# A hybrid attention layer on one core: the low parts of the in-projection's weights moved from GpSimd to VectorE

## The chip, the cores and the metric

The kernel runs on one core of one Trainium2 chip. The metric is device time in microseconds of one execution; a time given for a kernel is the median of its runs. The engines are TensorE (PE for matmuls, PEld for weight loads), VectorE (DVE), ScalarE (ACT), GpSimd (POOL) and SyncE (SP, which only issues DMAs here).

## The reference, cut to what matters

One layer of a diffusion backbone over 1024 latent tokens and 256 context tokens, model width 1024. One input projection feeds a gated DeltaNet group (four heads of 128) and a neighbourhood-attention group (eight heads of 64); both go through one output projection, a gated residual and a SwiGLU MLP.

```python
h = modulate(rms_norm(x, w1), shift1, scale1)        # latent and context tokens: T = 1280 rows of 1024
p = h @ w_in                                         # ONE combined in-projection: q, k, v, z, gates | q, k, v
oA = gated_deltanet(p[..., :DN_IN], conv_w, ...)     # short_conv + SiLU on q/k/v, chunked scan both ways
oB = neighbourhood_attention(p[..., DN_IN:], ...)    # QK RMSNorm, window keys + all context keys
x = x + gate1 * (concat(oA, oB) @ w_out)
x = x + gate2 * swiglu(modulate(rms_norm(x, w2), shift2, scale2))
```

Every large product is in float32, made on TensorE as three products of a reduced type: a number is split into a high part (the value rounded to the matmul's type) and a low part (the rest), and high·high, high·low and low·high are summed in PSUM. So each weight must be split once before TensorE can use it: one cast and one subtraction over the tile.

## The kernel before, in words

**Stages.** The profile shows four: the start and the normalization with the first two blocks of the in-projection (0 to 35 us), the rest of the in-projection with the preparation of the DeltaNet chunks running between it (35 to 560 us), the scans and the attention (560 to 780 us), and the output projection with the MLP (780 to 1509 us). The change is in the second.

**The in-projection** is a list of jobs (lines 1073 to 1082), taken in order by one loop (line 1095 on): the blocks k0 and k1 (computed together during the normalization), k2, k3, the wide tile z1, nk0 to nk2, the wide tile nv0, nk3, q0 to q3, nq0 to nq3, v0, the wide tile nv1, v1 to v3, and the wide tile z0. A `Block` makes 128 output columns for 1280 tokens (q and nq: 1024): for each of eight k-tiles, the three products in the order hi·hi, hi·lo, lo·hi (`mm_part`, L419), so the low part of the weights is needed only by the third group of matmuls of a block. A `Wide` tile makes 256 or 272 columns, token tile by token tile (L615).

**A block's weights.** `Block.prefetch` (L430) calls `load` (L191): a DMA on SP's queue into `wraw`, a cast on ACT into `whi` (L203), and `wlo = wraw - whi` (L204) on the engine `lo_engine`. There is one `wraw` buffer in this stage, and two each of `whi` and `wlo`. The next DMA waits until the subtraction has read `wraw`. The loop calls `jobs[n + 1].prefetch()` at the start of job n. A wide tile's weights go through the same `wraw` in two halves (L601 to L608): DMA, cast on ACT (L607), subtraction (L608, 128 x 1024 or 128 x 1088) into `zw`. Before the change GpSimd does 18 of the subtractions L204 and 8 of L608 in this stage. The block k0 names VectorE for its low part and k1 names GpSimd, in both kernels; the loads of the output projection name VectorE, in both.

**What else uses these engines.** VectorE does the short convolution: for the first four k blocks straight from PSUM (L461, accumulator `cacc`), after that from a copy in SBUF (L471, L475). It does the query-key norms (L516, L522, L529), the modulation's sums over DMA'd weights (`modulation`, L236 and L238 into `acc2`, which TensorE then reduces at L223), the recursion that inverts the diagonal blocks of all chunks (`block_inverses`, 30 steps of L916 and L918 on `N`; TensorE transposes `N` in and out at L906 and L928), and parts of the chunk preparation (`prep`: L1017, L1043). GpSimd does the diagonal extractions of the k blocks (L572 into `kd`, L577), the right-hand sides `rc` of the decay matrices (L871, used by TensorE at L884), and `rg` for the chunk preparation (L994, used at L1006).

**What sets the order.** The kernel is written in Tile: each engine's instruction order within the program is chosen by a scheduler that estimates when operands are ready, and semaphores are placed from it. So an instruction that changes its engine also changes where its neighbours stand, on all engines. Each engine runs its instructions strictly in order.

Of the kernel before, what the change touches and what calls it, by code (L numbers as in the profile page):

```python
# [9 lines left out]
F32 = mybir.dt.float32  # L10
# [4 lines left out]
OP = mybir.AluOpType  # L15
# [5 lines left out]
KT = 8  # L21
# [67 lines left out]
def hybrid(ctx, tc, a, dbg):  # L89
    nc = tc.nc  # L90
    pe, act, dve, pool, sp = nc.tensor, nc.scalar, nc.vector, nc.gpsimd, nc.sync
# [96 lines left out]
            dve.scalar_tensor_tensor(r, y, 1.5, r, op0=OP.add, op1=OP.mult)  # L188

    def weights(wp, raws=2, wide=132):  # L190
        def load(src, kt=KT, n=128, lo_engine=pool, raw=None, hi_engine=None):  # L191
            given = raw is not None
            if not given:
                raw = wp.tile([128, KT, wide], F32, name="wraw", tag="wraw", bufs=raws)
            hi = wp.tile([128, KT, 128], F32R, name="whi", tag="whi")
            lo = wp.tile([128, KT, 128], F32R, name="wlo", tag="wlo")
            r, h, o = raw[:, :kt, :128], hi[:, :kt], lo[:, :kt]
            if not given:
                sp.dma_start(r, src)
            if hi_engine:  # L200
                hi_engine.tensor_copy(h, r)
            else:
                act.copy(h, r)  # L203
            lo_engine.tensor_tensor(o, r, h.bitcast(F32), OP.subtract)  # L204
            return h, o
        return load
# [182 lines left out]
    with ExitStack() as bs:  # L389
# [32 lines left out]
        class Block:  # L422
# [4 lines left out]
                self.segs = SEGS[1:] if kind in ("q", "nq") else SEGS  # L427
                self.t0 = self.segs[0][0]

            def prefetch(self, raw=None, lo_engine=pool, hi_engine=None):  # L430
                i = self.i
                src = {"q": lambda: a["w_conv"][i], "k": lambda: a["w_conv"][4 + i], "v": lambda: a["w_conv"][8 + i],
                       "nq": lambda: a["w_nqk"][i], "nk": lambda: a["w_nqk"][4 + i]}[self.kind]()
                self.w = load_w(src, lo_engine=lo_engine, raw=raw, hi_engine=hi_engine)
# [149 lines left out]
        class Wide:  # L584
# [10 lines left out]
            def prefetch(self):  # L595
                h2, n = 2 * self.half, self.n // 2
                src = a["w_nv"] if self.kind == "nv" else a["w_z%d" % self.half]
                if self.kind == "z":
                    h2 = 0
                self.room()  # L600
                for i in range(2):  # L601
                    raw = wp.tile([128, KT, 136], F32, name="wraw", tag="wraw", bufs=1)
                    r, s = raw[:, :, :n], slice(i * n, i * n + n)
                    q = sp if self.half or self.kind == "nv" else act
                    with tc.issue_after(jobs[-3].last.ins) if i and q is act else ExitStack():
                        q.dma_start(r, src[h2 + i])
                        act.copy(self.hi[:, :, s], r)  # L607
                    pool.tensor_tensor(self.lo[:, :, s], r, self.hi[:, :, s].bitcast(F32), OP.subtract)  # L608

            def wide(self, t, c0, c1):  # L610
                p = bank("blk")
# [580 lines left out]
    with ExitStack() as gs:  # L1192
# [18 lines left out]
        def load(d, c, near):  # L1211

            def tile_of(name, src):
                t = sl.tile([128, 4, 128], F32, name=name, tag=name)
                sp.dma_start(fl(t), src)
                return t

            both = shared.pop(c, None)
            if both is None:
                r = slice(c * 128, (c + 1) * 128)  # L1220
                both = [tile_of("v", v_d[r]), tile_of("kt", k_d[r])]
                y = tile_of("y", fl(y_d[d, c]))
                both += [tile_of("kT", fl(kT_d[:, c])), tile_of("qT", fl(qT_d[:, c - 2])) if c >= 2 else None]
                if c in near:
                    shared[c] = both
            else:
                y = tile_of("y", fl(y_d[d, c]))
            at = tile_of("at", fl(at_d[d, c - 2])) if c >= 2 else None
            v, kt, kT, qT = both
            ready[d, c] = kT, qT, kt, v, y, at  # L1230
# [599 lines left out]
```

## Time and profile before

| | before |
|---|---|
| three runs | 1507.06, 1509.69, 1513.23 us (median 1509.69) |
| the profiled execution | 1510.77 us; its span 1509.0 us |
| PE busy in the span | 1458.9 us (97%) |
| DVE busy | 993.4 us (66%) |
| ACT busy | 704.0 us (47%) |
| POOL busy | 237.5 us (16%), 200 of them before 560 us |

How to read it: "busy" is the time in which the engine ran an instruction, so an instruction that is held up while it runs counts as busy for longer. A row of a group of instructions gives line, engine, operation, output and inputs, and durations in nanoseconds. A row of the waits names the engine, tile and line that waited, then the releaser, then the total, the count and the longest. A row of the timeline gives start, duration, engine, line, operation and operands, and in brackets the idle time ahead of it and what ended that.

### The profile page before, as it was taken

To read this page: it belongs to the slowest core of one execution; us is meant where nothing else is said; L and a number is where in the kernel's file an instruction comes from. 1 tells how busy PE (TensorE), PEld (TensorE's weight loads), DVE (VectorE), ACT (ScalarE), POOL (GpSimd) and SP (SyncE) were. 2 spreads that over 40 slices of the span, in tenths; PEclk is the share of its full clock that TensorE was granted. 3 is DMA by queue.
4 is the path that set the end of the run, shared out by engine and by line. 5 is a ranking of instruction groups with operands and counts; after the bars stand their busy time and mean duration, and the time that the engine had idled before them with its cause. 6 is when DMAs were issued, how large, how long until landed. Compare 5 with 4: busy or idle time off the path is not lost.

```text
span 1509.0 us, 23906 instructions
## 1 busy us (share of the span) xinstructions
PE 1458.9 (97%) x8702; PEld 1222.2 (81%) x8702; DVE 993.4 (66%) x1716; ACT 704.0 (47%) x1389; POOL 237.5 (16%) x286
## 2 busy tenths in 40 slices
PE   6999999999999998999999999999999999999998
PEld 3788797877788887888878888888888888888887
DVE  5773589865463745779867489765555567598652
ACT  5443442456663246667843284333333334354440
POOL 1154501455652201112210000000000000000000
PEclk9999999999999999999999999999999999999999
DMA  9274132778665558999539205333333335798742
GB/s 385 79 220 138 57 83 64 248 211 248 189 195 185 157 164 289 300 261 293 166 119 338 76 28 174 134 105 105 105 105 105 105 105 174 271 349 279 251 140 84
DMA packets 205398, 267.36 MB, mean 177 GB/s; under 512 B 15968, under 2 KB 113760, under 8 KB 204256
## 3 DMA queue, kind: packets, MB, share of 16 engines
q1 hardware_dynamic: 197680, 260.01, 53.5%
q10 hardware_dynamic: 7600, 5.81, 1.2%
q8 instruction: 69, 1.13, 0.3%
q14 instruction: 49, 0.40, 0.1%
HBM read 201.02 MB, written 68.94 MB: 179 GB/s over the span
## 4 chain that ended last, share of the span: by engine, by line
PE 51%; ACT 1%; DVE 1%; issue 0%; DVEq 0%
PE ps L1404 28%; PE ps L1747 14%; PE ps L1533 3%; PE ps L1381 1%; PE ps L1555 1%; PE sc L322 1%; PE sc L332 1%; PE sc L309 1%; DVE bt L313 0%; ACT sq L1308 0%; PE ps L1258 0%; ACT oacc L1325 0%; PE ps L223 0%; PE ps L1279 0%; PE ps L1284 0%
## 5 line engine op out<-in xcount | busy, mean ns | idle before, releaser
L1465 ACT CAST uhi<-wq 128x512 fp32r<-128x512 f32 x101 | 61.3, 622 | 135.4 <-issue 84.6
L419 PE MATMUL blk<-hh,whi 128*128 128x512 f32 (+1 forms) x410 | 121.2, 389 | 1.5 <-ACT kk L568 1.4
L1465 ACT CAST uhi<-ws 128x512 fp32r<-128x512 f32 x91 | 53.9, 621 | 146.6 <-PE ps L1404 92.1
L615 PE MATMUL blk<-zw,hh 128*128 128x256 f32 (+1 forms) x576 | 113.2, 291 | 1.0 <-ACT cr L467 1.0
L419 PE MATMUL blk<-hl,whi 128*128 128x512 f32 (+1 forms) x410 | 113.4, 370 | 0.3 <-DVE hl L735 0.3
L419 PE MATMUL blk<-hh,wlo 128*128 128x512 f32 (+1 forms) x410 | 112.5, 371 | 0.6 <-POOL wlo L204 0.6
L1466 DVE TENSOR_TENSOR ulo<-wq,uhi 128x512 fp32r<-128x512 f32 x101 | 67.6, 687 | 59.1 <-ACT uhi L1465 32.8
L1404 PE MATMUL ps<-hT,uhi 128*128 128x512 f32 x336 | 103.7, 390 | 0.0
L1404 PE MATMUL ps<-lT,uhi 128*128 128x512 f32 x336 | 103.5, 389 | 0.0
L1404 PE MATMUL ps<-hT,ulo 128*128 128x512 f32 x336 | 103.4, 389 | 0.0
L615 PEld LDWEIGHTS blk<-zw,hh 128*128 128x128 f32 x576 | 91.5, 190 | 4.2 <-ACT cr L467 1.4
L1404 PE MATMUL ps<-hB,uhi 128*128 128x512 f32 x288 | 89.1, 390 | 0.0
L1404 PE MATMUL ps<-lB,uhi 128*128 128x512 f32 x288 | 88.8, 389 | 0.0
L1404 PE MATMUL ps<-hB,ulo 128*128 128x512 f32 x288 | 88.6, 389 | 0.0
L419 PEld LDWEIGHTS blk<-hh,wlo 128*128 128x128 f32 x410 | 71.2, 189 | 14.8 <-POOL wlo L204 0.9
L419 PEld LDWEIGHTS blk<-hl,whi 128*128 128x128 f32 x410 | 71.3, 189 | 14.3 <-DVE hl L735 0.8
L615 PE MATMUL blk<-zw,hl 128*128 128x256 f32 (+1 forms) x288 | 82.3, 286 | 0.0
L419 PEld LDWEIGHTS blk<-hh,whi 128*128 128x128 f32 x410 | 67.9, 190 | 16.7 <-issue 3.8
L204 POOL TENSOR_TENSOR wlo<-wraw,whi 128x1024 fp32r<-128x1024 f32 x18 | 44.8, 2491 | 185.1 <-ACT whi L203 178.8
L1404 PEld LDWEIGHTS ps<-lT,uhi 128*128 128x128 f32 x336 | 63.1, 188 | 13.2
L1404 PEld LDWEIGHTS ps<-hT,ulo 128*128 128x128 f32 x336 | 63.1, 188 | 13.1
L1404 PEld LDWEIGHTS ps<-hT,uhi 128*128 128x128 f32 x336 | 62.9, 188 | 12.9
(361 smaller groups left out, 3499.3 us busy)
## 6 DMA issues: line engine op xcount, KB each, us to landing
wq<-w_fo SPq DMA_DIRECT2D x99, 256.0 KB, 4.4
wq<-w_gu SPq DMA_DIRECT2D x88, 256.0 KB, 2.9
wad<-wa SPq DMA_DIRECT2D x64, 256.0 KB, 4.2
bt<-rpb SPq DMA_DIRECT2D x64, 192.0 KB, 4.0
t_d<-g SPq DMA_DIRECT2D x22, 512.0 KB, 3.5
fr<-t_d SPq DMA_DIRECT2D x44, 256.0 KB, 4.9
f_d<-g SPq DMA_DIRECT2D x33, 256.0 KB, 2.1
fr<-f_d SPq DMA_DIRECT2D x33, 256.0 KB, 4.4
```

Source lines behind the costliest of these rows:

```text
L204: lo_engine.tensor_tensor(o, r, h.bitcast(F32), OP.subtract)
L309: s = pe.matmul(sc[:, u * 640 + n0:u * 640 + n1], q, ks[i], start=i == 0, stop=i == 1)
L322: pe.transpose(sc[:, u * 640 + j * 128:u * 640 + (j + 1) * 128], bt[:, j * 128:(j + 1) * 128], ident)
L332: return pe.matmul(sc[u * ND:u * ND + ND, 1280:1408], vv, pts[u][:, j * 128:(j + 1) * 128], start=j == 0, stop=j == 4)
L419: pe.matmul(o, ww[:, k], xx[k][:, s], start=k == 0 and j == 0, stop=k == KT - 1 and j == 2)
L615: pe.matmul(p[:, :c1 - c0], x[k][:, s], ww[:, k, c0:c1], start=k == 0 and j == 0, stop=k == KT - 1 and j == 2)
L1381: pe.matmul(o, w[wi][:, k], parts[xi][k][:, s], start=k == 4 and j == 0, stop=k == 3 and j == 2)
L1404: pe.matmul(o, w[wi][:, k], x[xi][:, k], start=first and k == 0 and j == 0, stop=k == n - 1 and j == 2, skip_group_check=True)
L1465: act.copy(hi, self.raw[key])
L1466: dve.tensor_tensor(lo, self.raw[key], hi.bitcast(F32), OP.subtract)
L1533: pe.matmul(o, w[wi][:, k], parts[xi][k][:, s], start=k == 0 and j == 0, stop=k == KT - 1 and j == 2)
L1747: pe.matmul(o[b], w[wi][:, b], F[xn, p][xi], start=n in (0, 1, 5) and p == 0 and j == 0, stop=p == NFB // 2 - 1 and j == 2, skip_group_che ...
```

## The change

In three places the engine of a weight subtraction becomes VectorE: the default of `load`, the default of `Block.prefetch`, and the subtraction of a wide tile. k1's explicit engine stays GpSimd.

```diff
-        def load(src, kt=KT, n=128, lo_engine=pool, raw=None, hi_engine=None):
+        def load(src, kt=KT, n=128, lo_engine=dve, raw=None, hi_engine=None):
...
-            def prefetch(self, raw=None, lo_engine=pool, hi_engine=None):
+            def prefetch(self, raw=None, lo_engine=dve, hi_engine=None):
...
-                    pool.tensor_tensor(self.lo[:, :, s], r, self.hi[:, :, s].bitcast(F32), OP.subtract)
+                    dve.tensor_tensor(self.lo[:, :, s], r, self.hi[:, :, s].bitcast(F32), OP.subtract)
```

So 26 instructions move: 18 of L204 and 8 of L608. The schedule follows, on every engine. Three places of it:

On VectorE, between the end of the second k block's convolution (`cacc_627`) and the start of the third's (`cacc_757`, from its first PSUM banks `blk_651` and `blk_652`); `wad` and `acc2_2262` belong to the first of the modulation's sums. Before:

```order
L461 SCALAR_TENSOR_TENSOR cacc_627<-blk_284,cw_73,cacc_627 128x512
L238 SCALAR_TENSOR_TENSOR acc2_2262<-wad_2280,sc2_100,acc2_2262 128x512
L238 SCALAR_TENSOR_TENSOR acc2_2262<-wad_2289,sc2_100,acc2_2262 128x512
L461 SCALAR_TENSOR_TENSOR cacc_757<-blk_651,cw_73,cacc_757 128x254
L238 SCALAR_TENSOR_TENSOR acc2_2262<-wad_2298,sc2_100,acc2_2262 128x512
L461 SCALAR_TENSOR_TENSOR cacc_757<-blk_651,cw_73,cacc_757 128x255
```

After, where `wlo_647` is the low part of the fourth k block's weights:

```order
L461 SCALAR_TENSOR_TENSOR cacc_627<-blk_284,cw_73,cacc_627 128x512
L204 TENSOR_TENSOR wlo_647<-wraw_645,whi_646 128x1024
L236 TENSOR_SCALAR acc2_2262<-wad_2258,sc2_100 128x512
L238 SCALAR_TENSOR_TENSOR acc2_2262<-wad_2260,sc2_100,acc2_2262 128x512
L238 SCALAR_TENSOR_TENSOR acc2_2262<-wad_2271,sc2_100,acc2_2262 128x512
L461 SCALAR_TENSOR_TENSOR cacc_757<-blk_651,cw_73,cacc_757 128x254
L461 SCALAR_TENSOR_TENSOR cacc_757<-blk_651,cw_73,cacc_757 128x255
```

The subtraction for the fourth block now stands on VectorE behind the last instruction of the first two blocks' 24 convolution steps, and the modulation's sums, which stood between the steps of the third block's convolution, stand ahead of them.

On GpSimd, at the decay matrices of the block inversion (`rc` from `GH` and `GL`, L871), the difference; rows with a minus are gone from this engine:

```order
 L871 TENSOR_TENSOR rc<-GL,cst 128x256
 L871 TENSOR_TENSOR rc<-GH,cst 128x512
-L204 TENSOR_TENSOR wlo<-wraw,whi 128x1024
 L871 TENSOR_TENSOR rc<-GL,cst 128x512
 L871 TENSOR_TENSOR rc<-GH,cst 128x512
 L871 TENSOR_TENSOR rc<-GL,cst 128x512
-L608 TENSOR_TENSOR zw<-wraw,zw 128x8x128
 L871 TENSOR_TENSOR rc<-GH,cst 128x256
 L871 TENSOR_TENSOR rc<-GL,cst 128x256
-L608 TENSOR_TENSOR zw<-wraw,zw 128x8x128
-L204 TENSOR_TENSOR wlo<-wraw,whi 128x1024 x5
```

Eight subtractions stood between and behind the right-hand sides; all are gone from GpSimd.

On TensorE, in the block whose weights are `whi_2557` and `wlo_2558` (q3, banks `blk_2694` and `blk_2695`), where the second modulation sum `acc2_2457` is reduced. Before:

```order
L419 MATMUL blk_2694<-hh0_129,wlo_2558 128x512
L419 MATMUL blk_2695<-hh0_129,wlo_2558 128x512
L223 MATMUL m_2714<-ones_61,acc2_2457 128x1 x4
L419 MATMUL blk_2694<-hh1_131,whi_2557 128x512
L419 MATMUL blk_2695<-hh1_131,whi_2557 128x512
```

After:

```order
L1009 MATMUL pr_2657<-mneg_597,mr_80 128x512
L419 MATMUL blk_2695<-hh2_133,wlo_2558 128x512
L223 MATMUL m_2714<-ones_61,acc2_2457 128x1 x4
L500 MATMUL m_2749<-ones_61,cr_2600 128x1 x8
L419 MATMUL blk_2694<-hh3_135,whi_2557 128x512
L419 MATMUL blk_2695<-hh3_135,whi_2557 128x512
```

The reduction stands two k-tiles of the block later, behind the products of the chunk preparation (`pr`) that came after it before.

## The prediction

> **What bounds the kernel now.** I read the page first, then the windows by stage, then TensorE's waits in the stage of the change, then the moved instructions and what runs beside them. From the page the span and the engines' busy time:
>
> ```profile
> span 1509.0 us, 23906 instructions
> PE 1458.9 (97%) x8702; PEld 1222.2 (81%) x8702; DVE 993.4 (66%) x1716; ACT 704.0 (47%) x1389; POOL 237.5 (16%) x286
> ```
>
> From the windows (stretch and its length in us, busy time and count of PE, PEld, DVE, ACT, POOL, then granted clock, DMA share, GB/s), the stage of the change, a part of it, and the two stages behind:
>
> ```profile
> 35.00:560.00 525.00, 507.09 (x3424) 430.68 (x3422) 337.50 (x435) 242.34 (x450) 194.90 (x207) 0.99 0.53 160
> 200.00:300.00 100.00, 97.19 (x575) 84.17 (x575) 93.53 (x93) 38.71 (x63) 19.28 (x18) 0.98 0.45 136
> 560.00:780.00 220.00, 205.13 (x1962) 180.11 (x1963) 164.74 (x508) 153.12 (x426) 34.20 (x69) 1.00 0.80 244
> 780.00:1509.00 729.00, 724.82 (x3210) 598.80 (x3209) 473.18 (x747) 288.09 (x489) 3.26 (x2) 1.00 0.47 160
> ```
>
> TensorE bounds. In the stage of the change it is idle 525 − 507.09 = 17.9 us, so 17.9 us is about the most that the change can bring, apart from TensorE's clock. Behind 560 us no instruction moves, and TensorE is busy 93 to 99% there, so a gain is carried to the end as it stands. TensorE's idle time in 35 to 560 us, by what it waited for (engine, tile and line; releaser; us in total, times, longest):
>
> ```profile
> PE pr L1030 <- DVE kk L1017: 2.3, 2, 1.9
> PE pr L1041 <- DVE y L1043: 1.9, 1, 1.9
> PE m L543 <- DVE cacc L461: 1.5, 1, 1.5
> PE m L928 <- DVE N L921: 1.3, 1, 1.3
> PE m L906 <- ACT N L908: 1.3, 1, 1.3
> PE m L223 <- DVE acc L238: 1.2, 1, 1.2
> PE m L884 <- POOL rc L871: 1.1, 3, 0.7
> PE blk L419 <- POOL wlo L204: 0.6, 1, 0.6
> PE m L928 <- DVE N L918: 0.3, 1, 0.3
> ```
>
> These sum to 11.5 us. Only 0.6 us is a wait for a moved instruction itself. If the change brings anything, it must come through its neighbours.
>
> **The change: the two engines' bills.** The moved instructions on GpSimd, and the same subtraction where VectorE does it already, later in the kernel and once at the start (group rows: busy us, mean ns; then min/median/max ns):
>
> ```profile
> L204 POOL TENSOR_TENSOR wlo<-wraw,whi 128x1024 fp32r<-128x1024 f32 x18 | 44.8, 2491 | 185.1 <-ACT whi L203 178.8 <-PE m L543 6.0
> L608 POOL TENSOR_TENSOR zw<-wraw,zw 128x1024 fp32r<-128x1024 f32 (+1 forms) x8 | 20.5, 2564 | 31.8 <-ACT zw L607 31.8
> L204 DVE TENSOR_TENSOR wlo<-wraw,whi x8: 1210/1214/1220, 685.9 to 846.5; 128x1024 fp32r<-128x1024 f32 x8
> L204 DVE TENSOR_TENSOR wlo<-fraw,whi x1: 1939/1939/1939, 20.3 to 20.3; 128x1024 fp32r<-128x1024 f32 x1
> ```
>
> GpSimd loses 44.8 + 20.5 = 65.3 us. VectorE gains 26 × 1.21 = 31.5 us, and each low part is ready 2.45 − 1.21 ≈ 1.2 us sooner if VectorE is free. But what VectorE does beside GpSimd's subtraction has a price now, as the timeline shows (start, duration, engine, line). Two pairs:
>
> ```profile
> 79.75 0.73 DVE L238 SCALAR_TENSOR_TENSOR acc<-wad,sc,acc 128x512 f32<-128x512 f32 x1
> 80.46 2.53 POOL L608 TENSOR_TENSOR zw<-wraw,zw 128x1088 fp32r<-128x1088 f32 x1 [4.75 <-ACT zw L607]
> 81.08 2.46 DVE L238 SCALAR_TENSOR_TENSOR acc<-wad,sc,acc 128x512 f32<-128x512 f32 x1
> 254.73 2.38 POOL L204 TENSOR_TENSOR wlo<-wraw,whi 128x1024 fp32r<-128x1024 f32 x1 [8.75 <-ACT whi L203]
> 254.91 2.57 DVE L916 TENSOR_TENSOR tt<-N 80x336 f32<-80x336 f32 x1
> 257.51 0.50 DVE L918 TENSOR_TENSOR N<-N,tt 80x336 f32<-80x336 f32 x1
> ```
>
> The same L238 takes 0.73 us alone and 2.46 beside GpSimd; the step L916 takes 2.57 beside it, and L918 of the same size 0.50 behind it. Both held instructions end within 0.6 us of GpSimd's end. So a subtraction on GpSimd costs VectorE (1.73 + 2.07) / 2 = 1.9 us when VectorE is at work on SBUF beside it. VectorE is busy 337.5 / 525 = 0.64 of the stage, so 26 × 0.64 × 1.9 = 31.6 us of its busy time are such stalls (an estimate; if steps that read PSUM are not held, less). 31.5 added against 31.6 removed: VectorE's bill stays about level. That is the centre of the forecast: GpSimd's work goes and VectorE's does not grow.
>
> [...]
>
> [...]
>
> **The change: which waits go.** Now the terms, each with its reason.
>
> Start of the stage: the convolution of the first k blocks, what TensorE needs, and what holds it (the group row is of 48 steps, two blocks' worth being 24 of the four blocks'):
>
> ```profile
> L461 DVE SCALAR_TENSOR_TENSOR cacc<-blk,cw,cacc 128x512 f32<-128x512 f32 (+4 forms) x48 | 28.4, 648 | 5.9 <-ACT cacc L452 5.8
> 64.47 1.05 ACT L203 CAST whi<-wraw 128x1024 fp32r<-128x1024 f32 x1 [1.74 <-PE blk L419]
> 83.08 0.74 PE L419 MATMUL blk<-hh,wlo 128*128 128x256 f32 x3
> 92.05 3.50 DVE L238 SCALAR_TENSOR_TENSOR acc<-wad,sc,acc 128x512 f32<-128x512 f32 x1
> 92.07 2.94 POOL L572 TENSOR_TENSOR kd<-kk,cst 128x1280 f32<-128x1280 f32 x1 [0.88 <-ACT kk L568]
> ```
>
> (T1) The third block's low part: ready 1.2 us sooner behind the cast at 64.47, the wait of 0.6 goes. (T2) L543 waits 1.5 for the end of the third block's convolution; an L238 of 3.50 us, held by GpSimd's L572, stood among its steps. In the new order the sums stand ahead and the convolution runs in one piece: 1.5 goes.
>
> The inversion. Around it GpSimd works in this order; and a query norm is held:
>
> ```profile
> 157.72 2.41 POOL L204 TENSOR_TENSOR wlo<-wraw,whi 128x1024 fp32r<-128x1024 f32 x1
> 166.85 2.38 POOL L608 TENSOR_TENSOR zw<-wraw,zw 128x1024 fp32r<-128x1024 f32 x1
> 182.35 2.39 POOL L204 TENSOR_TENSOR wlo<-wraw,whi 128x1024 fp32r<-128x1024 f32 x1 [5.25 <-ACT whi L203]
> 183.48 2.61 DVE L516 SCALAR_TENSOR_TENSOR cacc<-cacc,qkw,cr 128x1280 f32<-128x1280 f32 x1 [0.43 <-ACT cr L513]
> ```
>
> (T3) The right-hand sides `rc` stood behind the first two: 1.1 goes. (T4) L906 waits 1.3 for ACT's `N`, behind a VectorE chain in which L516 was held by about 1.3 us: 1.3 goes. (T5) In the recursion three GpSimd subtractions go and two VectorE ones enter: −3 × 2.07 + 2 × 1.21 = −3.8 us, so L928's 1.3 + 0.3 = 1.6 go. (T6) L223 stands two k-tiles later: 1.2 goes.
>
> The chunk preparation. Ahead of the L1017 for which L1030 waits, VectorE runs two L475 of the same size, the second beside GpSimd's subtraction; and one of two steps L529 that stand ahead of the L1043 for which L1041 waits:
>
> ```profile
> 297.19 1.30 DVE L475 SCALAR_TENSOR_TENSOR cacc<-cr,cw,cacc 128x1023 f32<-128x1023 f32 x1
> 299.05 2.39 POOL L204 TENSOR_TENSOR wlo<-wraw,whi 128x1024 fp32r<-128x1024 f32 x1
> 299.78 2.74 DVE L475 SCALAR_TENSOR_TENSOR cacc<-cr,cw,cacc 128x1023 f32<-128x1023 f32 x1
> 425.95 0.78 DVE L529 TENSOR_TENSOR hl<-cacc,hl 128x512 f16<-128x512 f32 x1
> ```
>
> (T7) Of the 2.3 the hold of 2.74 − 1.30 = 1.4 goes, and GpSimd's next `rg` come 2.4 sooner; I take 2.0. (T8) Both L529, some 0.75 each, stand behind the copies L1043 now: 1.5 of 1.9 goes. Sum: 0.6 + 1.5 + 1.1 + 1.3 + 1.6 + 1.2 + 2.0 + 1.5 = 10.8 us.
>
> TensorE's clock. In two short stretches it was granted half:
>
> ```profile
> 292.20:296.00 3.80, 3.80 (x11) 2.94 (x11) 3.51 (x4) 3.69 (x7) 3.80 (x4) 0.55 1.01 309
> 306.00:309.60 3.60, 3.60 (x20) 2.97 (x19) 3.08 (x4) 3.57 (x5) 3.54 (x4) 0.53 0.01 2
> ```
>
> They cost (1 − 0.55) × 3.8 + (1 − 0.53) × 3.6 = 3.4 us, and they follow right behind the waits of T6 and T7. Whether they go with these is not shown; I count half, 1.7.
>
> New waits. The order of TensorE is changed in 277 rows, and with twelve waits of mean 11.5 / 12 ≈ 1 us in the old one the new one will have some: I take three of 1.4 us (between that mean and the longest, 1.9), −4.2, for L1030, which stands three products earlier, and L1041 and L567, which follow it there. The tight place is the fourth block: VectorE reaches its low part behind the 24 steps of the first two, 28.4 / 2 = 14.2 us, that is at about 65.6 + 1.2 + 14.2 = 81.0 and ends at 82.2, against a need at 83.08 − 0.6 = 82.5. It fits by 0.3 us, so I price it at nothing, with 1 to 2 us if it slips.
>
> Sum: 10.8 + 1.7 − 4.2 = 8.3 us. Against its own time the profiled execution would go from 1510.77 to 1502.5; the median of the runs shown lies 1.08 lower, so **1509.69 − 8.3 = 1501.4 us**. Ends: all 10.8 and 3.4 and no new wait, 14.2, gives 1495.5; half the waits, no clock and 4.2 of new ones, 1.2, gives 1508.5.
>
> **Rivals.** (A) VectorE becomes the bound. In 200 to 300 us it is busy 93.5%, and five moved subtractions fall there: 5 × 1.21 = 6.1 us added. If the stalls are not given back there, T4 to T6 stay (4.1), the clock gives nothing, and the recursion's end moves by some 2 of the 6.1 that no idle time takes up: 10.8 − 4.1 − 4.2 − 2 = 0.5, so 1509 to 1510. For it: that busy share. Against it: a good part of it are the stalls. [...]
>
> (B) The gains are given back. TensorE reaches the next product sooner and waits there for the same producer: DMA, ACT, or the next VectorE step. Half of 10.8 with two new waits of 1.4 gives 2.6 to 3.2, so about 1506.5.
>
> (C) Slower: low parts come late at the starts of blocks. VectorE runs strictly in order; a low part stands behind whatever waits ahead of it, and the second half of a wide tile's stands on VectorE directly behind the first though its data come later (GpSimd idled 4.75 us for the cast ahead of the one at 80.46). If 16 of the 17 other block starts waited the 0.6 us that one did, that is 9.6; with 4.2 of new waits and half of the gains gone, 9.6 + 4.2 − 5 = 8.8, so 1518.5. It decides from where VectorE reaches a subtraction later than the block's third group of matmuls. Against it: weights are fetched a whole job ahead, and the stage's 22 jobs take 525 / 22 ≈ 24 us each.
>
> That the change does not do what it says is excluded by the order: 18 rows are gone from GpSimd and stand on VectorE, with the 8 of the wide tiles.
>
> **How the numbers follow.** Chances: forecast 0.60, A 0.15, B 0.17, C 0.08. No change is what lies within 0.5%, 7.5 us, about what a measurement here can tell from nothing. Of the forecast's 0.60 three quarters lie beyond that (45 of 60), with a little of B: faster 0.47. Slower is C, 0.08; the rest, 0.45, is the same. The range takes the forecast's ends with the runs' scatter of some 3 us: from 1494 to 1512, which holds A and B, and leaves C and the best end's tail out. The forecast's own range is 1495 to 1508.
>
> **What would show it.** Right: GpSimd's busy time falls to about 172 us while VectorE's stays within 10 us of 993; the mean of L238 comes close to 0.75; in TensorE's waits the nine rows above are gone or halved; the idle time in 35 to 550 us falls from 17.9 to about 10. Wrong: waits L419 for DVE `wlo` or L615 for DVE `zw` in the list (C); VectorE busy above 1010 with L928 or L906 waiting longer (A); the same idle total under other names, L1030, L1041 and L567 above all (B).

## The result, and the profile after

The changed kernel takes 1498.81 us (four runs, 1497.62 to 1501.48) against 1510.4 us (four runs, 1507.06 to 1513.23): a ratio of 0.9927, 95% interval 0.9911 to 0.9943, or 11.6 us less. The page and the windows of the changed kernel, by the same stages:

```profile
span 1495.5 us, 23900 instructions
PE 1454.9 (97%) x8702; PEld 1221.8 (82%) x8702; DVE 989.4 (66%) x1742; ACT 705.4 (47%) x1389; POOL 172.6 (12%) x260
...
35.00:560.00 525.00, 514.00 (x3530) 438.60 (x3529) 338.89 (x477) 251.61 (x469) 130.91 (x185) 0.99 0.55 168
200.00:300.00 100.00, 98.68 (x580) 85.69 (x580) 88.59 (x95) 38.56 (x66) 20.92 (x26) 0.97 0.46 140
35.00:550.00 515.00, 506.61 (x3462) 432.48 (x3461) 335.59 (x469) 246.42 (x456) 129.97 (x182) 0.99 0.55 165
```

GpSimd's busy time fell by 64.9 us and VectorE's by 4.0, though VectorE has 26 instructions more. In 35 to 550 us TensorE is idle 515 − 506.61 = 8.4 us, where before it was 515 − 497.37 = 17.6. Its waits in 35 to 550 us now:

```profile
PE m L543 <- DVE vt L547: 1.5, 1, 1.5
PE blk L419 <- ACT kk L568: 1.4, 1, 1.4
PE pr L1006 <- POOL rg L994: 1.2, 1, 1.2
PE m L508 <- ACT W L886: 1.0, 1, 1.0
PE blk L615 <- ACT cr L467: 1.0, 1, 1.0
PE m L848 <- DVE G L827: 0.4, 1, 0.4
PE sc L322 <- DVE bt L317: 0.4, 1, 0.4
PE blk L633 <- DVE zw L608: 0.4, 1, 0.4
```

None of the nine rows of the prediction is left. New are L1006 on `rg` (1.2), L508 (1.0, it was 0.2) and 0.4 for a wide tile's low part. The row of L322 belongs to the attention, which starts earlier in this window.

The two traces can be laid over each other: the n-th matmul of a line in one against the n-th in the other gives how far the changed kernel is ahead. At 61 us it is 0.55 behind (the start differs from run to run, below), at 86 us 0.5 ahead, at 147 us 1.7, at 173 us 3.6, at 200 us 4.4, at 261 us 6.5, at 346 to 386 us 9.4 to 9.1, at 477 us 12.4, and from 780 us to the end 13.5, unchanged (these are the two profiled executions; the medians lie 11.6 apart). So most of the gain is made between 61 and 480 us in six or seven steps, and kept; another 1.4 us comes at 548 us, where TensorE's granted clock was 0.57 (548 to 552 us) before the change; in the changed kernel it is 1.00 over 530 to 550 us.

What became of VectorE's work, in groups (busy us, mean ns) of the stage 35 to 560 us, first before:

```profile
L475 DVE SCALAR_TENSOR_TENSOR cacc<-cr,cw,cacc 128x1022 f32<-128x1022 f32 (+3 forms) x48 | 58.9, 1248 | 0.7
L238 DVE SCALAR_TENSOR_TENSOR acc<-wad,sc,acc 128x512 f32<-128x512 f32 x28 | 30.6, 1092 | 8.5 <-DMA wad<-wa 8.1
L916 DVE TENSOR_TENSOR tt<-N 80x120 f32<-80x120 f32 (+14 forms) x30 | 29.7, 989 | 7.1 <-ACT N L908 6.1
```

and after:

```profile
L475 DVE SCALAR_TENSOR_TENSOR cacc<-cr,cw,cacc 128x1022 f32<-128x1022 f32 (+3 forms) x48 | 48.5, 1044 | 0.5
L916 DVE TENSOR_TENSOR tt<-N 80x120 f32<-80x120 f32 (+14 forms) x30 | 25.4, 847 | 7.1 <-ACT N L908 6.2
L204 DVE TENSOR_TENSOR wlo<-wraw,whi 128x1024 fp32r<-128x1024 f32 x18 | 22.8, 1269 | 20.1 <-ACT whi L203 20.1
L238 DVE SCALAR_TENSOR_TENSOR acc<-wad,sc,acc 128x512 f32<-128x512 f32 x28 | 22.4, 802 | 7.2 <-DMA wad<-wa 6.7
L608 DVE TENSOR_TENSOR zw<-wraw,zw 128x1024 fp32r<-128x1024 f32 (+1 forms) x8 | 10.3, 1287 | 6.5 <-ACT zw L607 6.4
```

The same 48 + 28 + 30 instructions take 10.4 + 8.2 + 4.3 = 22.9 us less. Take for each of VectorE's instructions in the stage what it took beyond the shortest of its line and shape in the traces; call this excess a hold where GpSimd ran beside it. Then 32.1 us of excess stood beside the moved subtractions before (48 instructions beside one, 18 of them held over 0.5 us), and 22.8 + 10.3 = 33.1 us of work came in. The recursion's step that took 2.57 us, and the fourth block's low part, on the timeline of the changed kernel:

```profile
80.89 1.21 DVE L204 TENSOR_TENSOR wlo<-wraw,whi 128x1024 fp32r<-128x1024 f32 x1
...
248.30 0.50 DVE L916 TENSOR_TENSOR tt<-N 80x336 f32<-80x336 f32 x1
248.83 0.50 DVE L918 TENSOR_TENSOR N<-N,tt 80x336 f32<-80x336 f32 x1
```

### The profile page after: what moved, and what is told of

Same layout as the page of the kernel before. It is cut to its first block, busy times and chain, and to the rows that moved or that the text cites. A ratio compares the mean times of both kernels' runs of the same rounds, so it can differ in the third digit from the quotient of the medians.

```text
span 1495.5 us, 23900 instructions
## 1 busy us (share of the span) xinstructions
PE 1454.9 (97%) x8702; PEld 1221.8 (82%) x8702; DVE 989.4 (66%) x1742; ACT 705.4 (47%) x1389; POOL 172.6 (12%) x260
## 4 chain that ended last, share of the span: by engine, by line
PE 51%; ACT 1%; DVE 1%; issue 0%; DVEq 0%
PE ps L1404 28%; PE ps L1747 14%; PE ps L1533 3%; PE ps L1381 2%; PE ps L1555 1%; PE sc L309 1%; PE sc L322 1%; PE sc L332 1%; DVE bt L313 0%; ACT sq L1308 0%; PE ps L1258 0%; ACT oacc L1325 0%; PE ps L223 0%; PE ps L1279 0%; PE ps L1284 0%
## 5 line engine op out<-in xcount | busy, mean ns | idle before, releaser
L313 DVE CUSTOM_DVE_ANT_0 bt<-sc,bt 128x640 f32<-128x640 f32 x64 | 52.3, 820 | 28.2 <-issue 9.1
```

What stands on the lines that cost most here:

```text
L313: dve.tensor_tensor_reduce(bt, sc[:, u * 640:u * 640 + 640], bt, -1.0, 3.0e38, OP.add, OP.min, m[:, 0:1])
```

## The experiments

Five accounts of the 11.6 us were told apart. H: GpSimd's subtractions hold VectorE while they run, and that is what costs. Q: GpSimd's queue, which delays `rc` and `rg`. W: the raw weight tile is freed sooner, so ScalarE's casts wait less for the next weights. O: the scheduler's new order by itself. L: each low part is ready 1.2 us sooner. Each experiment is timed against the kernel before on the same chip.

**The two halves of the change.** e1_blocks: the first two edits of the diff alone. e2_wide: the third alone.

> Only the 18 low parts of the blocks move to VectorE; the 8 of the wide tiles stay on GpSimd. Theory H (VectorE is held by GpSimd's subtractions, and that is what goes): of the 32.1 us of holds in the trace of before, those beside L204 go, about two thirds (18 of 26 instructions), so two thirds of the 11.6 us: 7 to 9 us faster than before, about 1502. Rival L (what counts is the low part's own latency, 1.2 us sooner): no block waits for it but the third, 0.6 us, so within 2 us of before. Rival O (the schedule's new order by itself): no price follows from the count of moved instructions; anything from 0 to 12.

> Only the 8 low parts of the wide tiles move. Theory H: a third of the holds go, 3 to 4 us faster than before, about 1507, with the second third of the inversion's waits (rc behind a wide tile's subtraction) gone. Rival L: no wait for a wide tile's low part stands in the list of before, so no change. If e1_blocks and e2_wide sum to the 11.6 us, the parts do not depend on each other.

e1_blocks: 1501.2 against 1511.2 us, 0.9934 (0.9921 to 0.9948), so 10 us. e2_wide: 1506.71, 0.9969 (0.9956 to 0.9981), so 4.5. Both lie somewhat above what H expected, and L, which expected at most 2 us from the first and nothing from the second, is out; the sum of 14.5 us is 3 over the whole, about what the intervals (2 us each way) allow. In e2_wide TensorE's executed order is row for row that of before, and VectorE's differs in 4 rows beside the moved ones, so O has little part in its 4.5 us. The blocks alone leave a wait for the wide tile's low part on GpSimd (L608 takes 2.94 us on average there, 1.29 on VectorE in the changed kernel), which the change does not have:

```profile
PE blk L633 <- POOL zw L608: 2.1, 1, 2.1
```

**GpSimd kept busy behind VectorE.** e4_shadow and e5_memset make the change and add, after each subtraction on VectorE, GpSimd work of the old length over the raw tile.

```diff
             lo_engine.tensor_tensor(o, r, h.bitcast(F32), OP.subtract)
+            if raws == 1 and not given:                                   # e4_shadow, and alike in Wide
+                pool.tensor_tensor(r, h.bitcast(F32), h.bitcast(F32), OP.subtract)
+            if raws == 1 and not given:                                   # e5_memset, and alike in Wide
+                for x in (r, r, r[:, :4]):
+                    pool.memset(x, 0.0)
```

> The changed kernel, and behind each of the 26 subtractions on VectorE GpSimd makes one of the same size (the high part minus itself, from two SBUF inputs, over the raw tile that is no longer needed). The low parts stay where the change put them. Theory H: VectorE has the 32 us of work and about 32 us of holds again, so the gain is lost: 1508 to 1518. Rival L: the low parts are as soon as in the changed kernel, 1499 to 1502. Rival Q (what helped is GpSimd's queue, free for rc and rg): lost like in H.

> The same as e4_shadow, but GpSimd fills the raw tile with zeros two and a half times (three instructions of 1.0, 1.0 and 0.5 us by the rows of its fills, 0.52 us for 128x512), so that its queue is as long occupied and the raw tile as late free, without reading SBUF. Theory H: VectorE is not held, so 1499 to 1503, like the changed kernel. Rival Q (GpSimd's queue): 1506 to 1512, like e4_shadow. If fills hold VectorE as subtractions do, H expects what e4_shadow gives.

e4_shadow: 1515.81 us, 1.0039 (1.0025 to 1.0054). e5_memset: 1516.18, 1.0037 (1.0023 to 1.0051). Both lose everything, so e5 is against H as I had put it. VectorE was held 27.4 us beside e4's subtractions but only 7.0 beside e5's fills. e4's executed order is that of the changed kernel but for two rows on TensorE and six on VectorE, so the new order does not bring the gain while GpSimd still subtracts. But both free the raw tile later than it ever was, 1.2 + 2.4 us after the cast instead of 2.4, and ScalarE's casts stood waiting for the DMA into it. Its waits in e5_memset:

```profile
ACT whi L203 <- DMA wraw<-w_nqk: 13.6, 4, 5.9
ACT zw L610 <- DMA wraw<-w_nv: 12.8, 3, 9.9
```

(before the change these two were 7.8 and 13.9, the longest 5.0 and 5.5), and in the changed kernel:

```profile
ACT zw L607 <- DMA wraw<-w_nv: 8.8, 3, 4.9
ACT whi L203 <- DMA wraw<-w_nqk: 3.8, 4, 1.5
```

Behind such a cast stand ScalarE's own results, and e5's new waits of TensorE are for these:

```profile
PE pr L1046 <- ACT kk L1038: 4.0, 2, 3.7
PE m L889 <- ACT W L891: 3.0, 1, 3.0
```

That e5 loses by these waits is argued, not tried: its order on TensorE also differs from the changed kernel's, in 106 rows. So this pair had two factors at once, and W had to be taken seriously. The next three were made to separate them.

**GpSimd kept busy ahead of VectorE, and the raw tile alone.** e9_oversub and e10_overfill put GpSimd's work into the low part's own tile, before the true subtraction, so that the raw tile would be freed as early as in the change; e11_rawlate only frees the raw tile late.

```diff
+        def over(o):                                                     # e9_oversub
+            x = hh[0][:, :1024].rearrange("p (k i) -> p k i", k=KT).bitcast(F32)
+            pool.tensor_tensor(o[:, :, :128], x, x, OP.subtract)
+        def over(o):                                                     # e10_overfill
+            for x in (o, o, o[:, :4]):
+                pool.memset(x.bitcast(F32), 0.0)
...
+            if raws == 1 and not given:                                  # e11_rawlate, and alike in Wide
+                pool.memset(r, 0.0)
```

> The changed kernel, and GpSimd first writes zeros into each of the 26 low-part tiles by a subtraction of the old size (two SBUF inputs, an operand that is constant in this stage), as soon as the tile is free; VectorE's true subtraction follows. The raw tile is freed as early as in the changed kernel, GpSimd's queue is occupied as before the change, and VectorE can be held. Theory H (holds): about 30 us of holds are back on VectorE, so 1506 to 1512. Theory W (the raw tile is freed 1.2 us sooner, so the next weights arrive sooner and ScalarE's cast holds up ScalarE's queue less: its waits for the raw tile's DMA were 40.2 us before, 26.5 after, 54.6 and 50.5 in e4_shadow and e5_memset, by the waits of ScalarE): nothing is lost, 1499 to 1502. Theory Q (GpSimd's queue): 1506 to 1512.

> As e9_oversub, with fills (two and a half per low part, 2.5 us) in place of the subtraction: the queue is occupied, the raw tile early, and VectorE hardly held (beside the fills of e5_memset it was held 7.0 us in all, beside the subtractions of before 32.1). Theory H: 1499 to 1503. Theory W: 1499 to 1502. Theory Q: 1506 to 1512, like e9_oversub.

> The changed kernel, and GpSimd fills the raw tile once (1.0 us) when VectorE has read it, so that the tile is freed about as late as before the change (1.2 + 1.0 against 2.4 us). Theory W: the gain is lost, 1506 to 1511. Theory H: no holds to speak of, 1499 to 1502. Theory Q: 26 us of the 65 are back in GpSimd's queue, so 2 to 4 us of the gain are lost, 1501 to 1503.

e11_rawlate: 1498.7 against 1511.56 us, 0.9918 (0.99 to 0.9937). Nothing is lost, though ScalarE's waits for the raw tile's DMA are back at 35.6 us, two thirds of the way from the changed kernel's 26.5 to the 40.2 of before, and though 26 us of GpSimd's queue are filled again: W falls, and the 2 to 4 us that Q expected to be lost did not show. What still later tiles cost, as in e4 and e5 (54.6 and 50.5 us of such waits), was not tried by itself.

e9_oversub: 1529.62 us, 1.0124 (1.0097 to 1.0151). e10_overfill: 1507.74 us, 0.9973 (0.9962 to 0.9983). The two differ by 22 us. As programs they differ in nothing but what GpSimd does for 2.1 or 2.5 us at a time: read two operands, or fill. But the scheduler made another order of each (by the traces, 232 rows of TensorE and 116 of VectorE differ), so the 22 us are not the price of the reading alone. The part 86 to 560 us of e9_oversub, then of e10_overfill:

```profile
86.00:560.00 474.00, 451.54 (x3024) 385.76 (x3023) 318.67 (x386) 214.58 (x401) 175.28 (x200) 0.98 0.53 160
```

```profile
86.00:560.00 474.00, 465.22 (x3187) 399.57 (x3185) 303.26 (x405) 222.57 (x422) 188.17 (x249) 0.99 0.56 168
```

GpSimd is busy 13 us longer with the fills; VectorE is busy 15 us longer beside the subtractions, with 19 instructions fewer done. Beside e9's subtractions VectorE was held 25.1 us, beside e10's fills 7.0.

Neither run went as I had written. In both, VectorE's subtraction has to wait until GpSimd has written the tile (first row: e9, second: e10), so the raw tile was not freed as early as in the change, and VectorE itself stood waiting. And e9 lies 18 us beyond the 1512 that H and Q gave as their upper end. It falls back 6.1 us at the third block, and later waits for the recursion and for GpSimd's `rg` (third and fourth row), so Q has a part in it:

```profile
DVE wlo L206 <- POOL wlo L418: 14.5, 6, 4.6
DVE wlo L206 <- POOL wlo L418: 10.8, 6, 3.6
PE m L936 <- DVE N L929: 5.0, 1, 5.0
PE pr L1014 <- POOL rg L1002: 4.4, 4, 2.2
```

e10 fell short of what H expected, 1507.7 instead of 1499 to 1503. Its loss stands at one place, the third block (k2). Its first waits, and then its timeline:

```profile
PE blk L425 <- DVE wlo L206: 3.9, 1, 3.9
PE blk L425 <- DVE cacc L468: 2.3, 1, 2.3
```

```profile
67.57 5.45 DVE L468 SCALAR_TENSOR_TENSOR cacc<-blk,cw,cacc 128x255 f32<-128x255 f32 x9
72.95 1.21 DVE L206 TENSOR_TENSOR wlo<-wraw,whi 128x1024 fp32r<-128x1024 f32 x1
...
74.21 1.43 PE L425 MATMUL blk<-hh,wlo 128*128 128x256 f32 x3 [3.86 <-DVE wlo L206]
```

In its order the third block's low part stands on VectorE behind nine steps of the convolution, and TensorE, which was ready for it at 74.21 − 3.86 = 70.35 us, gets it at 74.2. Between 61 and 86 us e10 falls 8.4 us back against the kernel before (0.5 ahead, then 7.9 behind). From 86 to 523 us it then gains 12.4 us (4.5 ahead), as the changed kernel does (0.5 to 12.5). So with GpSimd's queue as full as before the change, and hardly a hold, the later gain is whole. e9 loses a further 9.7 us over the same stretch, in its own order. The pair bears H out in direction; the run that tests it in one order is e12_fills, below.

**No low parts at all.** e3_none makes none of the 26 on either engine.

```diff
-                self.w = load_w(src, lo_engine=lo_engine, raw=raw, hi_engine=hi_engine)
+                self.w = load_w(src, lo_engine=lo_engine if raw is not None else None, raw=raw, hi_engine=hi_engine)
...
+            if lo_engine is None:
+                return h, h
...
-                self.hi, self.lo = w[:, 0], w[:, 1]
+                self.hi, self.lo = w[:, 0], w[:, 0]
```

> The 26 low parts are left out (the third product reads the high part again), on both engines; the raw tile is freed by the cast. It bounds what is left in the low parts after the change: VectorE has 32 us less to do and every weight is ready 1.2 us sooner. Theory H: VectorE's bill hardly counts in the changed kernel, since few of TensorE's waits name it: 1496 to 1499. Theory W: the raw tile is freed another 1.2 us sooner, so about as much again as a part of the gain, 1492 to 1497. If VectorE's 32 us had a price of their own, it would be far below, under 1490.

1493.37 us, 0.988 (0.9861 to 0.9899), 18 us below before: what is left in the low parts after the change is some 5 us (1498.81 − 1493.37 = 5.4), not 32. This lies below H's expectation and within W's, which e11 rules out; where the 5 us lie is said below.

**The old order without the holds.** e12_fills is the kernel before, with fills on GpSimd in place of the subtractions.

```diff
+            if raws == 1 and not given:
+                for x in (r, r[:, :4], o.bitcast(F32)):
+                    pool.memset(x, 0.0)
+                return h, o
             lo_engine.tensor_tensor(o, r, h.bitcast(F32), OP.subtract)
```

> The kernel before, in which each of the 26 subtractions on GpSimd becomes fills of the same length, 2.5 us (one and a half over the raw tile, one over the low part's, so the third product multiplies zeros). GpSimd's queue, the time at which the low part counts as made, and, but for a dozen rows, the order on TensorE and VectorE are those of the kernel before; VectorE makes no low part. What goes is that GpSimd reads SBUF beside VectorE. Theory H (the holds cost the time): 1495 to 1501, as good as the change or better, since VectorE does not get the 32 us of work either. Rival O (the schedule's new order is the gain): 1508 to 1512, no change. Rival Q (GpSimd's queue): 1508 to 1512.

1494.43 against 1510.51 us, 0.9883 (0.9858 to 0.9907): 16 us. Its stage, and GpSimd's fills:

```profile
35.00:560.00 525.00, 514.22 (x3557) 439.34 (x3549) 312.63 (x458) 254.25 (x482) 193.29 (x264) 1.00 0.56 171
```

```profile
L206 POOL MEMSET wraw<- 128x1024 f32 (+1 forms) x36 | 27.8, 773 | 25.4 <-ACT whi L203 24.4
L206 POOL MEMSET wlo<- 128x1024 f32 x18 | 17.7, 985 | 83.8 <-PE blk L423 83.7
```

GpSimd is as busy as before (193.29 against 194.90), TensorE's order differs in 4 rows and VectorE's in 12; what is gone is the reading beside VectorE (its holds there fall from 32.1 to 4.8 us), and 16 us go with it. That is H against O and against Q. Two things were not as I had written. The scheduler put the low part's fill ahead of the raw tile's, so the low part is ready sooner; of TensorE's waits before, that touches 0.6 us. And the raw tile is freed sooner, behind 1.5 us of fills: ScalarE's waits for it are 31.8 us against 40.2 before; e11, with 9 us more of them than the changed kernel, lost nothing by it.

**Place by place.** e6_early moves only the low parts of k2, k3 and z1.

```diff
+                if raw is None and (self.kind, i) in (('k', 2), ('k', 3)):
+                    lo_engine = dve
...
+                    e = dve if (self.kind, self.half) in (('z', 1),) else pool
```

> The kernel before, with only the low parts of k2, k3 and the wide tile z1 on VectorE (4 of 26). If the gain is made place by place, it is what TensorE gains up to 147 us in the changed kernel against the 61 us before: 1.72 + 0.55 = 2.3 us, so about 1508. If it comes from the schedule as a whole, the 4 instructions give anything from none to all of it.

1508.12 us, 0.9976 (0.9959 to 0.9993): 1 to 6 us, and in its trace 2.1 us are gained between 61 and 147 us. It bears the expectation out in size, but the interval is too wide to exclude much.

**The next holder.** After the change VectorE is still held beside the products `rg` (L994, 40 of them). e13_rg_dve moves these to VectorE as well, e14_rg_act to ScalarE.

```diff
-                            pool.tensor_tensor(rg, g, mle, OP.mult)
+                            dve.tensor_tensor(rg, g, mle, OP.mult)                                          # e13_rg_dve
+                            for h in range(4):                                                              # e14_rg_act
+                                act.activation(rg[:, h], M[C_LE + d], AF.Copy, scale=gg.bitcast(F32)[:, d, c, h:h + 1])
```

> The changed kernel, and the 40 products rg (L994) move from GpSimd to VectorE too. By the traces VectorE is held about 15 us beside them after the change, and TensorE waits 1.2 us for one; VectorE gets 40 x 0.7 = 28 us of work. Theory H: work against holds leaves VectorE's bill 10 us up, so within 2 us of the changed kernel, 1497 to 1501. If only the holds' timing counted: 1494 to 1497. If VectorE's added work counts in full there: 1502 and more.

> The changed kernel, and rg is made by ScalarE, four instructions of 128x128 for each of the 40. VectorE loses the 15 us of holds and gets nothing. Theory H: 1494 to 1498. Against it: ScalarE gets 160 instructions of about 0.25 us, some 40 us, in the stretch where it also evacuates PSUM for TensorE: if they stand ahead of evacuations, 1500 to 1506.

e13_rg_dve: 1493.99 us, 0.9882 (0.9858 to 0.9906), 16.5 us below before and some 5 below the changed kernel, whose interval (0.9911 to 0.9943) does not touch this one: a version that beats both. e14_rg_act: 1496.75, 0.9904 (0.9879 to 0.9929), not clear of the change. VectorE's rows in e13_rg_dve:

```profile
L994 DVE TENSOR_TENSOR rg<-GH,cst 128x512 fp32r<-128x512 f32 x20 | 13.9, 695 | 12.4 <-PE pr L1006 12.0 <-DMA x_d<-ut 0.3
L994 DVE TENSOR_TENSOR rg<-GL,cst 128x512 fp32r<-128x512 f32 x20 | 13.9, 695 | 0.0
L1017 DVE TENSOR_TENSOR kk<-kk,e 128x512 f32<-128x512 f32 x20 | 13.2, 695 | 2.7 <-ACT e L1014 2.7
```

L1017 took 1.07 us on average in the changed kernel (21.0 us in 20) and takes 0.695 here; the product itself takes 0.695 on VectorE where GpSimd took 1.35 to 1.41. VectorE's bill grew by 10 us in the stage, and the time fell. That is the lower end of what I had expected if "only the holds' timing" counted. By the laid-over traces 4.8 of the 6.3 us by which e13 is ahead of the changed kernel arise at one place, between 290 and 346 us, which the next section looks at.

## Why the prediction was right

The direction, the mechanism and the time's range held; the gain was 11.6 us where 8.3 was forecast. The range, 1494 to 1512, held the rivals A and B as well, so the time alone decides little; VectorE's bill, the waits that went and e12_fills decide.

**VectorE's bill.** 31.6 us of holds against 31.5 of work was forecast; 32.1 against 33.1 was found, and VectorE's busy time moved by 4 us of 993. The estimate came to 16.6 holds of 1.9 us; 18 of over 0.5 us were found, 1.8 on average. The moved subtractions themselves took 1.5 us beyond 1.21 and 1.23 each: L204 22.8 us where 18 x 1.21 is 21.8, L608 10.3 where 8 x 1.23 is 9.8. The trace of before showed the holds: in the prediction's two pairs VectorE's instruction ends 0.55 and 0.37 us behind GpSimd's and takes 2.46 and 2.57 us, where its like takes 0.73 and 0.50.

**The waits.** All nine went, 11.5 us where I took 10.8. By the laid-over traces, the first two (T1, T2) gave 1.1 and 1.2 us for 0.6 and 1.5; T3 1.9 for 1.1; T4 some 1.6 for 1.3; T5 2.2 for 1.6; T8 with its neighbours 3.2 (from 9.1 at 397 to 12.35 at 445 us) for 1.5, since two waits of 0.5 that I had left out went there too. T6 and T7, 3.2 us together, cannot be told from the clock and the new wait at L1006, which fall into the same place: 290 to 346 us brought 2.6 in all.

**The terms that were mis-sized** are the new waits and the clock. I took three new ones, 4.2 us, for L1030, L1041 and L567. What came is 1.2 for L1006 on `rg`, 0.8 more for L508, and 0.4 for L633, 2.4 us; none of the three lines I had named. The 1.8 us between explain over half of the 3.3 by which the forecast fell short; the rest lies in the terms above. Of the clock's 3.4 us I took half. In the changed kernel the two stretches that I meant did not go; they stand side by side in the same chunk preparation, behind the new wait of 1.2 us at L1006:

```profile
290.40:297.00 6.60, 6.60 (x26) 5.92 (x26) 4.11 (x5) 0.40 (x2) 6.48 (x6) 0.52 0.55 174
```

and a third one, at 548 us before, which I had not counted, is gone (1.4 us). So that term came out near its size by luck. In e13_rg_dve, where that wait is gone, the same stretch runs at full clock:

```profile
290.40:297.00 6.60, 6.60 (x54) 5.56 (x52) 6.50 (x11) 3.87 (x12) 6.13 (x9) 1.00 1.09 339
```

(1 − 0.52) x 6.6 = 3.2 us, most of the 5 us by which e13 is ahead. That the wait brings the half clock is a reading of the traces. All six kernels with a wait of 1.2 us or more for `rg` here (the changed one, e1, e4, e5, e9, e11) have 6.8 to 13.7 us of half clock behind it (in stretches of 4 us a granted 0.50 at 292 to 296 us in the changed kernel and e1, at 296 to 300 in e11); e3, e10, e12, e13 and e14, without it, have none here. But it was not tried by itself, and other waits do not decide it: L543, 1.5 us both times, has such a stretch behind it in before (546.9 us; 0.57 over 548 to 552) and none in the changed kernel (534.5 us; 1.00 over 532 to 540).

Why that `rg` came late can be read in the changed kernel's rows (the last is the same product alone):

```profile
284.67 1.49 POOL L994 TENSOR_TENSOR rg<-GH,cst 128x512 fp32r<-128x512 f32 x1
285.29 1.94 DVE L475 SCALAR_TENSOR_TENSOR cacc<-cr,cw,cacc 128x1022 f32<-128x1022 f32 x1
286.12 2.01 POOL L994 TENSOR_TENSOR rg<-GL,cst 128x512 fp32r<-128x512 f32 x1
288.19 0.50 PE L1006 MATMUL pr<-rg,mr 128*128 128x512 f32 x1 [1.25 <-POOL rg L994]
296.36 1.04 POOL L994 TENSOR_TENSOR rg<-GL,cst 128x512 fp32r<-128x512 f32 x1
```

The product takes 1.04 us alone and 1.49 and 2.01 here, 1.4 us more in the two, and TensorE waited 1.25. The first held VectorE's L475 (1.94 where it takes 1.28), and L475, under way when the second started, held that one. So here the hold went both ways; the prediction had drawn up its bill for VectorE alone.

**The tight place** fit: the fourth block's low part was forecast to start at 81.0 and end at 82.2, and ran from 80.89 to 82.10. VectorE ran the rows listed under the change in the order listed: behind the convolution's last step L204 at 80.89, L236 at 82.03, L238 from 82.54, L461 from 85.22 us. e10 shows the price when a low part does stand too far back, one block earlier: waits of 3.9 and 2.3 us and a granted clock of 0.80 over 60 to 86 us, 8.4 us in all, not the 1 to 2 that I had put on it. That is rival C's mechanism at one place, in another order.

**The rivals.** A (VectorE becomes the bound) failed on its own evidence: in 200 to 300 us VectorE was busy 93.53 before and 88.59 after, with the recursion inside; the busy share had in good part been holds. B (given back) did not show: TensorE's idle time fell from 17.6 to 8.4 us. C (late low parts) is one row of 0.4 us in the changed kernel. The move paid in this direction: a subtraction took 2.45 us on GpSimd, and of the 48 VectorE instructions beside one 18 were held, by 1.8 us on average; on VectorE it takes 1.21. The holds stand beside subtractions and hardly beside fills: 27.4 against 7.0 us in e4 and e5, 32.1 against 4.8 in before and e12.

**Where the other 5 us lie.** e3_none, e12_fills and e13_rg_dve end 3 to 6 us ahead of the changed kernel, and by the laid-over traces most of that, or more, arises between 290 and 346 us: the changed kernel gains 2.6 us there, e3 6.3, e12 6.8 and e13 7.4. It is the place of the late `rg` and the half clock behind it.

**What stays open** is why the same 31 us of VectorE's busy time are worth 16 us when they are holds (before against e12_fills, 993.4 to 962.1) and some 5 when they are work (the changed kernel against e3_none, 989.4 to 958.7). The one place above is most of the price of the work; why the holds cost three times as much no run here shows.

## What to carry to other kernels

Look on the timeline for VectorE instructions that take two or three times what their like take, and at what GpSimd runs beside them: here L238 took 2.46 us beside a GpSimd subtraction and 0.73 alone, and GpSimd's `rg` 2.01 us beside L475 and 1.04 alone, and no view names that as a wait, since the held engine counts as busy. Here VectorE did the moved work in half the time (1.21 us for 2.45), and its busy time stayed level (993.4 us, then 989.4) though it had looked full (93.53 of the 100 us from 200 to 300). After such a move check the new order for the place at which a product's operand now stands behind a long run of VectorE's queue. An experiment that adds a load must not lengthen a buffer's life or make another engine wait as well, or it tests two things; one that keeps the order of the instructions, as e12_fills does, is worth more than several that change it.

## What the runs showed of the hardware that was not expected

GpSimd's fills held VectorE hardly at all: 4.8 to 7.0 us beside 73 to 78 of VectorE's instructions in e5, e10 and e12, against 25 to 32 us beside 34 to 53 for subtractions (2.1 to 2.5 us each, the fills in place of one 2.5 together). GpSimd was held as well: in the changed kernel the 15 `rg` products of 1.04 us had, but for two, no VectorE instruction under way when they started, and each of the 25 longer ones (1.37 to 2.02 us) had. The convolution steps that read PSUM (L461) were not held: the 16 that ran beside a subtraction before were 0.1 us over their shortest in all. And the start, up to 61 us, differs from one profiled run to another by up to 4 us whatever the kernel (between 3.2 behind and 0.8 ahead of the run of before), with a stretch at half clock that begins between 24 and 29 us in 11 of the 14 (a granted 0.81 over 24 to 29 us in the changed kernel, 1.00 before); single profiles of kernels a few us apart are to be compared from 61 us on.
